# Second attention: one PSUM bank moves from the projections' ring to the ring of the turned probabilities, once the compressed branch's blocks are made

## The chip, the core and the metric

The kernel runs on one core of a Trainium2 chip. The metric is the device time of one execution in microseconds (us), the median of several runs. The core's engines work side by side and meet through semaphores: TensorE (PE in the profile; its weight loads are listed apart as PEld), VectorE (DVE), ScalarE (ACT), GpSimd (POOL) and the DMA queues, most of which SyncE (SP) issues. TensorE writes its results to PSUM, which has eight banks of 128 x 512 float32 here, b0 to b7; VectorE and ScalarE read them from there.

## The reference

Two transformer blocks on 512 tokens of width 1024, in float32. The first has a chunkwise mLSTM and a stick-breaking attention, mixed by gates, then a squared-ReLU MLP. The second is an attention with three branches (16 heads of 64 in 4 key groups); this is the part that the change touches. Cut to what matters:

```
def nsa_mixer(h, w_in, w_out, k_pos, k_w1, k_w2, v_pos, v_w1, v_w2, table):
    q, kv, g, z = split_cols(h @ w_in, [NSA_WIDTH, 6 * NSA_KV_WIDTH, 3 * H, 3 * NSA_WIDTH])
    k_c, v_c, k_s, v_s, k_w, v_w = [a.reshape(B, S, G, dh) for a in jnp.split(kv, 6, axis=-1)]
    gates = jax.nn.sigmoid(g).reshape(B, S, 3, H, 1)
    zs = jax.nn.silu(z).reshape(B, S, 3, H, dh)
    kc = compress_kv(k_c, k_pos, k_w1, k_w2)          # 31 blocks of 32 tokens: silu(flat @ w1) @ w2
    vc = compress_kv(v_c, v_pos, v_w1, v_w2)
    o_cmp, p_cmp = nsa_compressed(q, kc, vc, table)   # softmax over the 31 blocks
    sel = select_blocks(p_cmp, S)                     # the top min(16, 8) of 8 blocks: all
    o_slc = nsa_selected(q, k_s, v_s, sel, table)     # causal softmax with a bias by distance
    o_win = nsa_window(q, k_w, v_w, table)            # the same over a window of 512
    o = jnp.stack([o_cmp, o_slc, o_win], axis=2)
    y = jnp.sum(gates * o * zs, axis=2).reshape(B, S, NSA_WIDTH)
    return y @ w_out
```

The result is normalised, scaled and added to the block's input.

## The kernel before

Every weight product is split for accuracy: weights and activations are each held as a high part (float32r) and a low part, and a product is three matmuls, high by high, high by low and low by high (L332 to L334 and L365 to L367). Weights stream through `Weights._load` (L164): a DMA into `wr`, a cast to `wh` on ScalarE (L171), and the low part `wl` by VectorE or, from load 142 on, by GpSimd (L173).

The kernel runs in stages: the first mixer, the MLP, and `nsa` (L781), the second attention, which starts at about 875 us of the profiled execution. In `nsa` TensorE and GpSimd run in the order in which the program is written (L1392); VectorE, ScalarE and SyncE are put in order by the scheduler.

`nsa` divides the eight PSUM banks among four rings at L788. A ring hands out its banks in turn; a tile in a bank may be written by TensorE only once the last reader of the tile before it in that bank is done.

- `bank`, b0, b1, b7: the projections (`pj`, L792) and, as `mx` (L797), the compressed branch's small products: `cmp_middle`, `cmp_output`, `cmp_scores` (L1039) and `cmp_flip` (L1072).
- `sc`, b2 and b3: the score blocks of the selected and the window branch (L1211).
- `tp`, b4 and b5: the turned probabilities (`Unit.flip`, L1223), the turned gate rows (`gate_flip`, L1128), the gates spread over the rows (`gate_scale`, L1139) and the compressed branch's output (`finish`, L1086).
- `av`, b6: probabilities by values (`Unit.mix`, L1239).

`attention` (L1258) walks through 8 head pairs, 2 branches, 2 heads and 4 query blocks: 128 steps. A step issues two score matmuls (L1213, L1214). VectorE adds the bias and takes the row's minimum (L1216), and ScalarE takes the exponent (L1219). Two steps later TensorE turns the block by 1 to 4 transposes against the identity into a `tp` bank (L1233), ScalarE copies the high part to `ptall` (L1236) and VectorE the low part (L292). When two query blocks are turned, and two steps have passed, `mix` multiplies them by the values (L1249); its result is copied to `t` by ScalarE (L1255) and added up by VectorE (L292).

Between these pieces `Filler` (L187) issues other work on TensorE in portions: the projections that later heads need (`gen_t`, 8 portions of three matmuls, L332 to L334), read after the last portion by ScalarE and VectorE (L991 and L289 for `z`; L874 and L289 for queries; L852 for keys). `early` (L1005) makes the compressed keys and values first; its last lines are

```
                yield from weave(keys(2), {2: middle, 5: lambda: output(1)})
                spread_values(0)
                spread_values(1)
```

after which the compressed branch's blocks are made. `combine(p)` (L1168) then goes through the head pairs: three `z` projections each, and at set portions the compressed branch's scores (`cmp_scores`, half a group at a time), their softmax and `cmp_flip`. `gate_flip`, `gate_scale` and `finish` are jobs that the filler issues as soon as their inputs are ready. After the last head pair the remaining flips, mixes and jobs are issued, and then the output projection (L365 to L367).

Of the kernel before, what the change touches and what calls it, by code (L numbers as in the profile page):

```python
# [8 lines left out]
F32 = mybir.dt.float32  # L9
# [6 lines left out]
T = 512  # L16
# [235 lines left out]
def tile_blocks(ctx, tc, x, xt, wts, prm, cst, table, post_g, w2k, w2v, out):  # L252
# [6 lines left out]
    banks = ctx.enter_context(tc.tile_pool(name="banks", bufs=1, space=PSUM))  # L259

    def ring(*ids):
        turn = [0]

        def take():
            i = ids[turn[0] % len(ids)]
            turn[0] += 1
            return banks.tile([128, T], F32, name=f"b{i}", tag=f"b{i}", bufs=1)
        return take
# [512 lines left out]
    def nsa(x2, ssq2):  # L781
# [3 lines left out]
        kst, qst = {}, {}  # L785
        with ExitStack() as pts:
            pt = pts.enter_context(tc.tile_pool(name="pt", bufs=1))
            bank, sc, tp, av = ring(0, 1, 7), ring(2, 3), ring(4, 5), ring(6)  # L788

            opened, when, used = [0], [0], [0]  # L790

# [2 lines left out]
                when[0] = fill.ticks  # L794
                return bank()

            mx = bank  # L797

            acts = [act_tiles(kt) for kt in range(KT)]

# [64 lines left out]
            def keys(gq):  # L865
                return gen_t(pj, acts, keys_evac(gq))
# [12 lines left out]
            def queries(m):  # L879
                return gen_t(pj, acts, queries_evac(m))  # L880
# [48 lines left out]
            def cmp_hidden(Fs, st):  # L929
                hp = pj()  # L930
                for k4 in range(4):
                    wh, wl = W.next()
                    Fh, Fl = Fs[k4]
                    for jj in range(4):
                        a = wh[:, 256 * jj:256 * jj + 256]
                        b = wl[:, 256 * jj:256 * jj + 256]
                        o = hp[:, 0:256]
                        pe.matmul(o, Fh[:, jj, :], a, start=(k4 == 0 and jj == 0), stop=False)
                        pe.matmul(o, Fh[:, jj, :], b, start=False, stop=False)
                        pe.matmul(o, Fl[:, jj, :], a, start=False, stop=(k4 == 3 and jj == 3))  # L940
                    if k4 < 3:
                        yield 1300.0
                th = pt.tile([128, 256], F32, name="th", tag="z", bufs=ZB)
                s.activation(th, hp[:, 0:256], AF.Tanh, scale=0.5)
                stt(th, th, 1.0, hp[:, 0:256], OP.add, OP.mult)
                st["th"] = th
                yield 1300.0

            def cmp_middle(th):
                pst = mx()  # L950
                for k in range(2):
                    pe.transpose(pst[:, 128 * k:128 * k + 128], th[:, 128 * k:128 * k + 128], ident)
                hT = pt.tile([128, 256], F32, name="hT", tag="z", bufs=ZB)
                ts(hT, pst[:, 0:256], 0.5)
                return hT
# [3 lines left out]
            def cmp_output(i, hT, w2):  # L959
                o = mx()  # L960
                for k in range(2):
                    if i == 0:
                        pe.matmul(o[:, 0:128], w2[:, k, :], hT[:, 128 * k:128 * k + 128],
                                  start=(k == 0), stop=(k == 1))
                    else:
                        pe.matmul(o[:, 0:64], hT[:, 128 * k:128 * k + 128], w2[:, k, :],
                                  start=(k == 0), stop=(k == 1))
                if i == 0:
                    hi_lo(kc[:, :, 0, :], kc[:, :, 1, :], o[:, 0:128].rearrange("p (g c) -> p g c", g=4))
                else:  # L970
                    vc = w2t[:, 1, 0:64]
                    v.tensor_copy(vc, o[:, 0:64])
                    tc.keep_in_program_order(g.memset(vcb, 0.0))
                    pct["v"] = vc

            def spread_values(gq):
                vc = pct["v"]
                for r in range(4):
                    o = vcb[32 * r:32 * r + 32, gq, r // 2, 64 * (r % 2):64 * (r % 2) + 64]
                    (s.copy, v.tensor_copy)[r % 2](o, vc[32 * gq:32 * gq + 32, :])  # L980

            def project(p, br):
                if (p, br) in zt:
                    return
                while live[0] == ZB:
                    yield None
                live[0] += 1
                z = pt.tile([128, T], F32, name="z", tag="z", bufs=ZB)

                def evac(ps):  # L990
                    s.activation(z, ps, AF.Tanh, scale=0.5)  # L991
                    stt(z, z, 1.0, ps, OP.add, OP.mult)
                yield from gen_t(pj, acts, evac)
                zt[p, br] = z
# [4 lines left out]
            def weave(gen, hooks):  # L999
                for k, ns in enumerate(gen):  # L1000
                    yield ns
                    if k in hooks:
                        hooks[k]()

            def early():  # L1005
                st = {}

                def middle():
                    st["hT"] = cmp_middle(st["th"])

                def output(i):
                    cmp_output(i, st["hT"], st[i])
                Fs, st[0] = yield from compress(0)
                yield from both(cmp_hidden(Fs, st), project(0, 0))
                Fs, st[1] = yield from compress(1, ({2: middle}, {2: lambda: output(0)}))
                started[0] = True
                yield from both(cmp_hidden(Fs, st), queries(4))
                yield from weave(keys(2), {2: middle, 5: lambda: output(1)})
                spread_values(0)
                spread_values(1)  # L1020

            def both(a, b):
                for k, ns in enumerate(b):
                    yield ns
                    if k % 2 == 1:
                        try:
                            yield next(a)
                        except StopIteration:
                            pass
                yield from a  # L1030
# [321 lines left out]
            for br in range(2):  # L1352
                values(br)
            load_near(0)
            fill.add(early(), 57200.0)
            attention(fill)
            fill.finish()
# [34 lines left out]
    with tc.manual_schedule(engines={mybir.EngineType.PE, mybir.EngineType.Pool}):  # L1392
        nsa(xb, sums2)
# [55 lines left out]
```

## Time and profile before

| what | value |
|---|---|
| median of 3 runs | 1371.41 us (1369.96 to 1372.78) |
| the profiled execution's own time | 1371.08 us |
| its span in the profile | 1369.4 us |
| PE busy | 1324.5 us (97%) |
| PEld busy | 1091.6 us (80%) |
| DVE, ACT, POOL busy | 720.9, 655.6, 273.8 us |
| chain of waits that ended last | PE 70%, issue 15%, DVE 8%, ACT 4% |

The profile's instruction rows give the start in us from the span's start, the duration, the engine, the line of the program, the operation, out<-in by the program's names, the shapes and how many were merged into the row; in brackets stands the engine's idle time just before, with what ended it. Matmuls are pipelined: the ends of those rows are modelled and lie behind the start of the next one, so a wait of TensorE is read best from start to start. [...]

### The profile page before, as it was taken

The numbers are of one execution on the slowest core, as the hardware profiler recorded it, in microseconds if no ns is written. First come the engines' busy times: TensorE is split into PE (matmuls) and PEld (weight loads), VectorE is DVE, ScalarE is ACT, GpSimd is POOL, SyncE is SP. The second block draws the span as 40 slices with busy tenths as digits, with TensorE's granted clock in tenths as the row PEclk, the third lists the DMA queues.
The fourth block names the chain that finished last, engine by engine and source line by source line (L and its number), as shares of the span: only waits on it lengthen the run. The fifth ranks groups of instructions, "written<-read, shape, count | busy, mean of one in ns | idle before, by whom it ended". The sixth has DMA issues, their size and how long they took to land.

```text
span 1369.4 us, 17872 instructions
## 1 busy us (share of the span) xinstructions
PE 1324.5 (97%) x6670; PEld 1091.6 (80%) x6670; DVE 720.9 (53%) x1354; ACT 655.6 (48%) x1281; POOL 273.8 (20%) x243
## 2 busy tenths in 40 slices
PE   9999999999999999999999999999889999999998
PEld 7977887777786888888888888888767788888776
DVE  4589435656567535342233322544775766665623
ACT  6588624544434316351135512345556566665532
POOL 0023101110101000000000000145536344335342
PEclk9999999999999999999999999999999999999999
DMA  7411231223131424862333224313313112222132
GB/s 236 139 46 48 77 93 51 88 62 93 47 107 47 154 62 133 122 186 92 95 102 96 93 92 125 126 60 124 100 49 113 50 62 65 68 62 62 47 109 77
DMA packets 40694, 125.30 MB, mean 92 GB/s; under 512 B 4528, under 2 KB 9184, under 8 KB 40352
## 3 DMA queue, kind: packets, MB, share of 16 engines
q1 hardware_dynamic: 39696, 119.98, 28.0%
q0 software_dynamic: 912, 4.19, 2.3%
q8 instruction: 52, 0.85, 0.3%
q14 instruction: 34, 0.28, 0.1%
HBM read 115.77 MB, written 8.39 MB: 91 GB/s over the span
## 4 chain that ended last, share of the span: by engine, by line
PE 70%; issue 15%; DVE 8%; ACT 4%; POOL 2%; DMA 1%; POOLq 0%; DVEq 0%; SPq 0%; ACTq 0%
PE b L365 10%; PE b L367 10%; PE b L366 10%; PE b L332 10%; PE b L333 9%; PE b L334 9%; PE b L1249 2%; PE b L1233 2%; PE b L1213 1%; PE b L1214 1%; PE b L828 1%; DVE ptall L292 1%; ACT P L1219 1%; DVE b L1216 1%; POOL ssr L292 1%
## 5 line engine op out<-in xcount | busy, mean ns | idle before, releaser
L171 ACT CAST wh<-wr 128x1024 fp32r<-128x1024 f32 (+3 forms) x204 | 207.7, 1019 | 404.6 <-PE b L367 225.1
L332 PE MATMUL b<-ah,wh 128*128 128x512 f32 x808 | 332.1, 411 | 2.6 <-ACT w2t L852 2.2
L173 DVE TENSOR_TENSOR wl<-wr,wh 128x1024 fp32r<-128x1024 f32 (+2 forms) x142 | 169.4, 1194 | 297.1 <-ACT wh L171 296.6
L334 PE MATMUL b<-ah,wl 128*128 128x512 f32 x808 | 317.4, 393 | 0.0
L333 PE MATMUL b<-al,wh 128*128 128x512 f32 x808 | 317.2, 393 | 0.0
L173 POOL TENSOR_TENSOR wl<-wr,wh 128x1024 fp32r<-128x1024 f32 (+1 forms) x62 | 141.6, 2289 | 190.3 <-ACT wh L171 166.3
L334 PEld LDWEIGHTS b<-ah,wl 128*128 128x128 f32 x808 | 152.3, 189 | 32.6
L332 PEld LDWEIGHTS b<-ah,wh 128*128 128x128 f32 x808 | 152.8, 189 | 30.3 <-ACT w2t L852 2.5
L333 PEld LDWEIGHTS b<-al,wh 128*128 128x128 f32 x808 | 153.0, 189 | 25.5 <-issue 1.9
L365 PE MATMUL b<-wh,ah 128*128 128x512 f32 (+3 forms) x352 | 126.1, 360 | 1.9 <-ACT wh L171 1.9
L366 PE MATMUL b<-wl,ah 128*128 128x512 f32 (+3 forms) x352 | 125.8, 357 | 0.0
L367 PE MATMUL b<-wh,al 128*128 128x512 f32 (+3 forms) x352 | 125.8, 357 | 0.0
L1219 ACT ACTIVATE P<-b,nm 128x128 f32<-128x128 f32 (+3 forms) x128 | 67.6, 528 | 77.8 <-DVE nm L1216 73.7
L367 PE MATMUL b<-wh,hl 128*128 128x512 f32 x256 | 101.2, 396 | 0.0
L366 PE MATMUL b<-wl,hh 128*128 128x512 f32 x256 | 101.2, 395 | 0.0
L365 PE MATMUL b<-wh,hh 128*128 128x512 f32 x256 | 101.2, 395 | 0.0
L292 DVE TENSOR_TENSOR ptall<-b,ptall 128x128 fp32r<-128x128 f32 (+3 forms) x128 | 62.4, 489 | 65.1 <-ACT ptall L1236 64.3
L1216 DVE CUSTOM_DVE_ANT_0 b<-b,bt 128x128 f32<-128x128 f32 (+3 forms) x128 | 63.2, 495 | 28.0 <-PE b L1214 27.7
L365 PEld LDWEIGHTS b<-wh,ah 128*128 128x128 f32 x352 | 66.6, 190 | 9.8 <-ACT wh L171 2.1
L367 PEld LDWEIGHTS b<-wh,al 128*128 128x128 f32 x352 | 66.7, 189 | 8.5 <-DVE al L289 0.3
L366 PEld LDWEIGHTS b<-wl,ah 128*128 128x128 f32 x352 | 66.8, 190 | 8.2
L292 POOL TENSOR_TENSOR rsr<-rsm,mhalf 128x2 f32<-128x2 f32 (+1 forms) x3 | 2.4, 806 | 336.4 <-DVE rsm L286 336.4
(301 smaller groups left out, 2153.6 us busy)
## 6 DMA issues: line engine op xcount, KB each, us to landing
wr<-in_wts_dram SPq DMA_DIRECT2D x188, 512.0 KB, 3.6
bt_d<-tr POOLq DMA_DIRECT2D x4, 768.0 KB, 21.6
wr<-in_wts_dram SPq DMA_DIRECT2D x8, 280.0 KB, 2.6
xk<-in_xt_dram SPq DMA_DIRECT2D x8, 256.0 KB, 3.9
xn<-in_x_dram SPq DMA_DIRECT2D x4, 512.0 KB, 4.7
xbig<-in_x_dram SPq DMA_DIRECT2D x1, 2048.0 KB, 9.8
x_d<-xbig SPq DMA_DIRECT2D x8, 256.0 KB, 2.8
bt<-bt_d SPq DMA_DIRECT2D x8, 256.0 KB, 3.2
```

Of the source, the lines that this page charges most:

```text
L171: nc.scalar.copy(hi, raw)
L173: eng.tensor_tensor(lo, raw, hi.bitcast(F32), OP.subtract)
L292: (eng or v).tensor_tensor(out_, a, b, op)
L332: pe.matmul(o, a, ah, start=(kt == 0), stop=False)
L333: pe.matmul(o, a, al, start=False, stop=False)
L334: pe.matmul(o, b, ah, start=False, stop=(kt == KT - 1))
L365: pe.matmul(o, ah[:, tsl], a, start=(kk == 0 and k == 0), stop=False)
L366: pe.matmul(o, ah[:, tsl], b, start=False, stop=False)
L367: W.last = pe.matmul(o, al[:, tsl], a, start=False, stop=end)
L1216: v.tensor_tensor_reduce(S[:, 0:n], S[:, 0:n], self.bt[:, h % 2, 512 - n:512], 1.0, -NEG, OP.add, OP.min, nm)
L1219: latest[0] = s.activation(P[:, 0:n], S[:, 0:n], AF.Exp, bias=nm, scale=-1.0, accum_out=self.dn[:, tb, br, h % 2:h % 2 + 1])
L1233: pe.transpose(pst[:, 128 * sb:128 * sb + 128], P[:, 128 * sb:128 * sb + 128], ident)
```

## The change

```
-            bank, sc, tp, av = ring(0, 1, 7), ring(2, 3), ring(4, 5), ring(6)
+            sc, av = ring(2, 3), ring(6)
+            ids = {"bank": [0, 1, 7], "tp": [4, 5]}
+            given = {"bank": -1, "tp": -1}
+
+            def from_ring(name):
+                i = given[name] = (given[name] + 1) % len(ids[name])
+                return banks.tile([128, T], F32, name=f"b{ids[name][i]}", tag=f"b{ids[name][i]}", bufs=1)
+
+            def bank():
+                return from_ring("bank")
+
+            def tp():
+                return from_ring("tp")
+
+            def regroup():
+                last = ids["bank"][given["bank"]]
+                ids["bank"] = [0, 1]
+                given["bank"] = last if last < 2 else 0
+                ids["tp"] = [4, 5, 7]
...
-            mx = bank
+            def mx():
+                return bank() if len(ids["bank"]) == 3 else tp()
...
                 yield from weave(keys(2), {2: middle, 5: lambda: output(1)})
                 spread_values(0)
                 spread_values(1)
+                regroup()
```

Until `regroup` runs, at the end of `early`, the rings are as before. From then on the projections have two banks, b0 and b1; the `tp` ring has three, b4, b5 and b7, and also takes the compressed branch's scores and turned blocks (`cmp_scores`, `cmp_flip`). The number of instructions and, on TensorE, GpSimd and SyncE, their order are unchanged. On ScalarE and on VectorE one instruction moves ahead of a neighbour, at one place some ten us after `early`: the copy of a turned block (L1236) ahead of an exponent (L1219), and that block's low part (L292) between the two adds of a compressed score. Everything else is the bank that a tile lies in.

TensorE's order at the end of `early` before: the last portion of the keys of group 2 (tile 8641 in b0), a turned block, then the next projection, tile 8746; the digit behind b is the bank, the number behind it the tile.

```order
L334 MATMUL b0_8641<-ah7_6869,wl_8473 128x512
L1233 MATMUL b5_8726<-ident_65,P_8620 128x128 x2
L332 MATMUL b0_8746<-ah0_6855,wh_8533 128x512
L333 MATMUL b0_8746<-al0_6856,wh_8533 128x512
L334 MATMUL b0_8746<-ah0_6855,wl_8534 128x512
```

The same place with the change (line numbers from the rings on are 18 to 20 higher):

```order
L334 MATMUL b0_8641<-ah7_6869,wl_8473 128x512
L1253 MATMUL b5_8726<-ident_65,P_8620 128x128 x2
L332 MATMUL b1_8746<-ah0_6855,wh_8533 128x512
L333 MATMUL b1_8746<-al0_6856,wh_8533 128x512
L334 MATMUL b1_8746<-ah0_6855,wl_8534 128x512
```

Before, tile 8746 takes the bank of the keys that were finished just ahead of it; now it takes b1, whose last tile was the compressed values' turned hidden layer.

TensorE before at the first two `finish` products (L1088, of head pairs 0 and 1), with one portion of a projection and one turned block between them:

```order
L1088 MATMUL b5_9109<-pct_9093,vcb_6871 128x512
L332 MATMUL b7_9077<-ah3_6861,wh_8742 128x512
L333 MATMUL b7_9077<-al3_6862,wh_8742 128x512
L334 MATMUL b7_9077<-ah3_6861,wl_8743 128x512
L1233 MATMUL b4_9116<-ident_65,P_9013 128x128 x2
L1088 MATMUL b5_9121<-pct_9093,vcb_6871 128x512
```

and with the change:

```order
L1108 MATMUL b4_9109<-pct_9093,vcb_6871 128x512
L332 MATMUL b0_9077<-ah3_6861,wh_8742 128x512
L333 MATMUL b0_9077<-al3_6862,wh_8742 128x512
L334 MATMUL b0_9077<-ah3_6861,wl_8743 128x512
L1253 MATMUL b5_9116<-ident_65,P_9013 128x128 x2
L1108 MATMUL b7_9121<-pct_9093,vcb_6871 128x512
```

Before, the second product reuses b5 after one other `tp` tile; now two other `tp` tiles lie between two uses of a bank.

TensorE before at the attention's end: the last two turned blocks, the turned gate rows of head pair 7 (L1131), the first half of the last mix, the first spread gate (L1141), the mix's second half:

```order
L1233 MATMUL b5_11471<-ident_65,P_11406 128x128 x3
L1233 MATMUL b4_11477<-ident_65,P_11431 128x128 x4
L1131 MATMUL b5_11484<-ident_65,gz_6877 128x128 x4
L1249 MATMUL b6_11491<-ptall_6876,vst_6874 128x256
L1249 MATMUL b6_11491<-ptall_6876,vst_6874 128x128
L1249 MATMUL b6_11491<-ptall_6876,vst_6874 128x256
L1249 MATMUL b6_11491<-ptall_6876,vst_6874 128x128
L1141 MATMUL b4_11496<-gT_11489,gsel_6879 128x512
L1249 MATMUL b6_11491<-ptall_6876,vst_6874 128x256 x3
```

and with the change:

```order
L1253 MATMUL b7_11471<-ident_65,P_11406 128x128 x3
L1253 MATMUL b4_11477<-ident_65,P_11431 128x128 x4
L1151 MATMUL b5_11484<-ident_65,gz_6877 128x128 x4
L1269 MATMUL b6_11491<-ptall_6876,vst_6874 128x256
L1269 MATMUL b6_11491<-ptall_6876,vst_6874 128x128
L1269 MATMUL b6_11491<-ptall_6876,vst_6874 128x256
L1269 MATMUL b6_11491<-ptall_6876,vst_6874 128x128
L1161 MATMUL b7_11496<-gT_11489,gsel_6879 128x512
L1269 MATMUL b6_11491<-ptall_6876,vst_6874 128x256 x3
```

The gate rows' tile 11484 follows tile 11471 in b5 before; now b5 last held an earlier turned block, and 11471 lies in b7.

## Rows read from the trace of the kernel before

**Rows 1.** Waits of TensorE, 1054 to 1318 us: line, releaser, total us, times, longest.
```profile
PE b L332 <- ACT w2t L852: 2.2, 1, 2.2
PE b L1233 <- DVE ptall L292: 1.9, 5, 0.7
PE b L1131 <- DVE ptall L292: 1.8, 1, 1.8
PE b L1088 <- DVE z L292: 0.9, 1, 0.9
PE b L1141 <- DVE ptall L292: 0.8, 1, 0.8
PE b L1141 <- DVE z L292: 0.4, 1, 0.4
```
**Rows 2.** Windows: length, busy of PE, PEld, DVE, ACT, POOL, PEclk, DMA share, GB/s.
```profile
1054.00:1318.00 264.00, 255.44 (x1453) 214.11 (x1452) 170.29 (x428) 159.23 (x394) 102.29 (x59) 0.99 0.20 58
1056.90:1062.30 5.40, 5.40 (x35) 4.77 (x35) 5.22 (x8) 4.70 (x11) 1.69 (x1) 1.00 0.36 102
1316.00:1320.00 4.00, 4.00 (x17) 3.50 (x17) 1.86 (x3) 0.58 (x1) 3.15 (x3) 0.71 0.43 98
```
**Rows 3.** Timeline of TensorE around the wait at 1102 us.
```profile
1101.12 0.39 PE L333 MATMUL b<-al,wh 128*128 128x512 f32 x1
1101.35 0.40 PE L334 MATMUL b<-ah,wl 128*128 128x512 f32 x1
1102.42 0.33 PE L1233 MATMUL b<-ident,P 128*128 128x128 f32 x1 [0.67 <-DVE ptall L292]
1102.51 0.48 PE L1141 MATMUL b<-gT,gsel 128*128 128x512 f32 x1
```
**Rows 4.** Timeline of TensorE at the end of `early` and seven us later.
```profile
1054.05 0.38 PE L1233 MATMUL b<-ident,P 128*128 128x128 f32 x2
1056.66 0.50 PE L332 MATMUL b<-ah,wh 128*128 128x512 f32 x1 [2.24 <-ACT w2t L852]
...
1063.44 0.57 PE L1249 MATMUL b<-ptall,vst 128*128 128x256 f32 x4
```
**Rows 5.** Timeline of ScalarE at the same place.
```profile
1055.08 1.04 ACT L171 CAST wh<-wr 128x1024 fp32r<-128x1024 f32 x1
1056.03 0.58 ACT L852 COPY w2t<-b 128x512 f32<-128x512 f32 x1
```
**Rows 6.** Timeline of VectorE: the add that empties b6.
```profile
1061.62 0.68 DVE L292 TENSOR_TENSOR t<-t,b 64x512 f32<-64x512 f32 x1
```
**Rows 7.** Timeline of TensorE at the attention's end.
```profile
1310.86 0.94 PE L1233 MATMUL b<-ident,P 128*128 128x128 f32 x7
1313.64 0.66 PE L1131 MATMUL b<-ident,gz 128*128 128x128 f32 x4 [1.84 <-DVE ptall L292]
1314.05 0.65 PE L1249 MATMUL b<-ptall,vst 128*128 128x256 f32 x4
1314.97 0.79 PE L1141 MATMUL b<-gT,gsel 128*128 128x512 f32 x1 [0.27 <-ACT gT L1133]
...
1318.66 0.40 PE L365 MATMUL b<-wh,yh 128*128 128x512 f32 x1
```
**Rows 8.** Timelines of VectorE and ScalarE at the attention's end.
```profile
1312.31 0.69 DVE L292 TENSOR_TENSOR t<-t,b 64x512 f32<-64x512 f32 x1
1313.03 1.16 DVE L292 TENSOR_TENSOR ptall<-b,ptall 128x384 fp32r<-128x384 f32 x2
...
1311.85 0.95 ACT L1236 CAST ptall<-b 128x384 fp32r<-128x384 f32 x2
...
1314.33 0.59 ACT L1133 CAST gT<-b 128x512 fp32r<-128x512 f32 x1 [1.53 <-PE b L1131]
```
**Rows 9.** Timelines of VectorE and TensorE: a projection's last read, that bank's next opening.
```profile
1133.53 0.69 DVE L289 SCALAR_TENSOR_TENSOR q<-b,q 64x512 fp32r<-64x512 f32 x1
...
1139.31 0.48 PE L332 MATMUL b<-ah,wh 128*128 128x512 f32 x1
```

## The prediction

> **What bounds the kernel now.** I read the windows first, then TensorE's waits, then the timeline around each wait. In the stretch that the change can touch, from the end of `early` to the output projection, TensorE is busy in 255.4 of 264 us, VectorE in 170 and ScalarE in 159 [rows 2]. So TensorE's own order sets the pace, and only what makes it wait can be won. Its waits are few [rows 1]: ten in six groups, 8.0 us of idle time together, all of them for ScalarE or VectorE to finish with a tile. The reader is to see that each first line named is one that opens a PSUM bank: the first portion of a projection (L332), a turned block (L1233), turned gate rows (L1131), a `finish` product (L1088) or a spread gate (L1141). The score blocks (L1213) and the mixes (L1249) are not in the list. Nine of the ten stand in the `tp` ring of two banks, and the tenth in the projections' ring.
>
> The idle time of a row is smaller than what the wait costs. A matmul of 512 columns lasts 0.39 us in the rows, but the next starts 0.23 us after it [rows 3]; seven transposes take 0.94 us, so 0.11 us from one to the next with a last one of 0.27 [rows 7]. In both cases 0.16 us of the earlier row overlaps what would have followed. A wait therefore costs its idle time and 0.16 us. The check is the wait at 1102.42: 1.07 us after the start before it instead of 0.23, which is 0.84, against 0.67 + 0.16.
>
> **The change part by part.** No instruction is added or taken away and TensorE's order stands, so the sum is made of waits that go, shrink or appear.
>
> 1. The projection after `early`. It waits 2.24 us because the ring's turn gives it the bank of the keys just finished, whose copy (L852) stands behind a weight cast on ScalarE and ends at 1056.61 [rows 4, 5]. Cost 2.40 us. With b1, long read, it can follow the transposes. What is late next is the mix at 1063.44: it opens b6, which VectorE frees at 1062.30 [rows 4, 6]. VectorE is busy 5.22 of the 5.40 us ahead of that [rows 2], with the keys' low parts, which wait for the same copy as before, so it won't be earlier. The mix can start 0.05 us later, at 1062.35, and the gain is 1.1 us. Bounds: 1.1, if VectorE keeps its queue, and 2.4, if it makes room; I take 1.1, since the row shows no room.
>
> 2. Five turned blocks, 1.9 us idle, 1.9 + 5 x 0.16 = 2.7 us. With three banks each has a tile's time more. One of the five is not won: the block at 1102.42 gets b4, and the spread gate 0.09 us behind it gets b5 and so the same low part to wait for [rows 3]. Of that wait's 0.83 us only 0.09 remains. Sum 2.7 - 0.83 + 0.09 = 1.96.
>
> 3. One `finish` product, 0.9 + 0.16 = 1.06 us [rows 1]: it waited for VectorE to multiply the `finish` product before it, in the same bank; now it takes b7.
>
> 4. Two spread gates, 0.8 + 0.4 + 2 x 0.16 = 1.52 us [rows 1], won in the same way.
>
> 5. The end. The turned gate rows wait for the low part of a block that shares their bank, 1.84 us [rows 7]. With the change they follow the seven transposes: start 1310.86 + 7 x 0.11 = 1311.63, end of the four at about 1312.3. What is late next is the first half of the mix, since VectorE frees b6 at 1312.31 + 0.69 = 1313.00 [rows 8]: start 1313.05 instead of 1314.05. ScalarE is free at 1312.80 and copies the gate rows in 0.59, until 1313.39 [rows 8]; the spread gate follows at 1313.5, the second half of the mix needs the last low part, ready at 1313.03 + 1.16 = 1314.19, for its last four matmuls, and ends with the second spread gate at about 1314.7. The fourth matmul of the output projection, at 1318.66 before [rows 7], comes at 1314.95 + 0.70 = 1315.65: 3.0 us won. [...] With the change 0.75 us of waiting is left there, as much as in waits of rows 1 after which the clock did not fall: over the whole stretch its mean is 0.99, and the hundredth, 2.6 us of the 264, is about the end's own. Bounds: 1.3 if the clock falls all the same, 3.0 if not; I take 3.0.
>
> Nothing is costed for the rest, with these covers. A projection's evacuation has 5.1 us to spare with two banks at the tightest of 25 openings: the queries read last at 1134.22 are followed in b1 by the opening at 1139.31 [rows 9]. The cost if that cover is gone is rival C. The compressed scores and turned blocks now pass through `tp`; each holds a bank for a few us more, beside a third bank, and behind them in TensorE's queue stand portions and scores for which ScalarE waits: rival B. The instruction that moves on ScalarE and VectorE issues nothing and goes past one neighbour.
>
> [...]
>
> Sum: 1.1 + 1.96 + 1.06 + 1.52 + 3.0 = 8.6 us. The profiled execution took 1371.08 us (span 1369.4 and 1.7 around it), 0.3 under the median, so I take the sum off the median: 1371.4 - 8.6 = **1362.8 us**. Gains add up because VectorE and ScalarE, busy less than two thirds of the stretch, are mostly started by TensorE and move forward with it.
>
> **The rivals.**
>
> A. The waits are passed on. As at 1102 us, the next instruction may need what the same queue on VectorE delivers late, and a third bank would only move the wait. For it: the row itself, and that VectorE is full for whole stretches like 1056.9 to 1062.3 [rows 2]. Against it: after the other waits the next bank needed is one read earlier. Then the eight waits of steps 2 to 4 bring 0.09 us each, 0.7, with 1.1 for the first and 1.3 at the end: 3.1 us, 1368.3 us.
>
> B. Slower through the compressed branch: its eight scores and four turned blocks wait in `tp` behind low parts that VectorE delivers late, where in the old ring they found banks read long before. If each waits as the block at 1102 us did, 12 x 0.84 = 10 us, and a few flips wait behind them for another 2: 1371.4 - 8.6 + 12 = 1375 us. It decides once VectorE is later than two turned blocks, about 4 us, at such a place. Against it: the `tp` waits of now are at most 0.87 us with two banks.
>
> C. Slower through the projections: 25 openings that wait as the `finish` product did, 1.03 us each, 26 us: 1371.4 - 8.6 + 26 = 1389 us. It decides when an evacuation lasts 5 us longer than in rows 9. [...] The trace shows the clock to stay at 0.99 through the waits of now [rows 2].
>
> That the change does not do what it says I leave out: the banks in TensorE's order are as the ring says.
>
> **How the numbers follow.** Forecast 0.76, A 0.16, B 0.05, C 0.03. The forecast's own range comes from its bounds: step 1 may bring 1.3 more, the end 1.7 less, and some waits of steps 2 to 4 (4.5 us) may be passed on: 1361 to 1366. To hold 8 in 10 the range reaches toward A and leaves half of it, B and C outside: 1360.5 to 1367.5. A measurement of this kernel can tell 0.2%, 2.7 us, from no change. The forecast lies beyond that, A (3.1 us) on its edge: 0.08 of it faster, 0.08 the same. Of B 0.03 is slower, 0.02 the same, C is slower. Faster 0.84, same 0.10, slower 0.06.
>
> **What would show it.** In the changed profile the waits of L332, L1088 and L1131 (by their old numbers) are gone from TensorE's list between `early` and the output projection, and what is left there is under 3 us; the mix seven us after `early` is late for b6, and a spread gate waits where the block at 1102 us did; the clock stays at 1.00 around the attention's end. Wrong would be: new waits at compressed scores (B) or at first portions of projections (C), or a list with as much idle time under other lines (A).

## The result, and the profile after

| | before | changed |
|---|---|---|
| median | 1372.01 us (1369.96 to 1372.78, 4 runs) | 1362.43 us (1362.11 to 1363.05, 4 runs) |
| ratio | | 0.9931, 95% interval 0.9919 to 0.9944 |
| span of the profiled execution | 1369.4 us | 1360.4 us |
| mean granted clock | 0.993 | 0.995 |

The changed kernel is 9.6 us faster; the forecast was 8.6 less than 1371.4, 1362.8 us. The two profiled executions differ by 9.0 us (1371.08 and 1362.11), which is what the starts below add up to; the medians differ by more, with four runs of the kernel before spread over 2.8 us. Lines 788 and later have moved: L1233 (turned block) is now L1253, L1213 (score) L1233, L1249 (mix) L1269, L1131 (gate rows) L1151, L1141 (spread gate) L1161, L1088 (product of `finish`) L1108, and the compressed scores and turned blocks are L1066 and L1096.

TensorE's list of waits from `early` to the output projection, in the columns of [rows 1], has two lines left, 2.7 us:

```profile
PE b L1269 <- DVE t L292: 2.1, 2, 1.3
PE b L1161 <- DVE ptall L292: 0.6, 1, 0.6
```

The list of the kernel before has seven lines, with eleven waits and 8.3 us. [rows 1] shows six of them; the seventh is the first spread gate at the end, which waits for its own input ([rows 7] has it at 1314.97):

```profile
PE b L1141 <- ACT gT L1133: 0.3, 1, 0.3
```

The windows of that stretch and of the attention's end, against [rows 2]: nine microseconds less for the same matmuls (1453 and 1454 records), and the clock at the end (PEclk, the share of TensorE's full speed that was granted) is 1.00 instead of 0.71.

```profile
1054.00:1309.00 255.00, 252.25 (x1454) 213.11 (x1453) 169.41 (x427) 158.76 (x394) 101.30 (x58) 1.00 0.20 60
...
1307.00:1311.00 4.00, 3.99 (x23) 3.43 (x24) 3.01 (x5) 0.63 (x2) 2.15 (x2) 1.00 0.31 82
```

At the end of `early` [rows 4] the projection follows the transposes, and the mix seven microseconds later waits. Below it is the add on VectorE that empties its bank [rows 6]: it ends at 1062.39, and the mix starts at 1062.44, as worked out (1062.35).

```profile
1054.10 0.38 PE L1253 MATMUL b<-ident,P 128*128 128x128 f32 x2
1054.24 0.48 PE L332 MATMUL b<-ah,wh 128*128 128x512 f32 x1
...
1062.44 0.67 PE L1269 MATMUL b<-ptall,vst 128*128 128x256 f32 x4 [1.28 <-DVE t L292]
```

```profile
1061.71 0.68 DVE L292 TENSOR_TENSOR t<-t,b 64x512 f32<-64x512 f32 x1
```

Where the block of 1102.42 waited [rows 3], the block no longer waits, and the spread gate behind it does. Nothing is won (0.83 us at the block, 0.84 lost again at the gate); the prediction, which worked out that this wait is passed on, left 0.09:

```profile
1098.95 0.27 PE L1253 MATMUL b<-ident,P 128*128 128x128 f32 x1
1099.87 0.47 PE L1161 MATMUL b<-gT,gsel 128*128 128x512 f32 x1 [0.65 <-DVE ptall L292]
```

The attention's end, against [rows 7]: the gate rows start 0.78 us after the seven transposes do, where 2.78 us passed before, and the mix is the one that waits.

```profile
1304.63 0.95 PE L1253 MATMUL b<-ident,P 128*128 128x128 f32 x7
1305.41 0.60 PE L1151 MATMUL b<-ident,gz 128*128 128x128 f32 x4
1306.82 0.67 PE L1269 MATMUL b<-ptall,vst 128*128 128x256 f32 x4 [0.81 <-DVE t L292]
1307.50 0.47 PE L1161 MATMUL b<-gT,gsel 128*128 128x512 f32 x1
1307.81 1.04 PE L1269 MATMUL b<-ptall,vst 128*128 128x256 f32 x8
1308.68 0.44 PE L1161 MATMUL b<-gT,gsel 128*128 128x512 f32 x1
...
1309.67 0.39 PE L365 MATMUL b<-wh,yh 128*128 128x512 f32 x1
```

TensorE runs the same matmuls in the same order in both kernels, so each start can be set against its own start before. In the stretch the difference grows from nothing (-0.05 us at 1054) to 9.01 us, in some fifteen steps:

| step of the prediction | forecast, us | measured, us, from starts in the two profiles |
|---|---|---|
| 1 projection after `early` | 1.1 | 2.48 won, 1.55 given back at the mix: 0.93 |
| 2 five turned blocks | 1.96 | 0.59 + 0.83 - 0.84 + 0.53 + 0.35 + 0.43 = 1.89 |
| 3 product of `finish` | 1.06 | 1.13 |
| 4 two spread gates | 1.52 | 1.01 + 0.63, less 0.18 at a compressed score 3 us behind the first: 1.46 |
| not counted: 1184.84 and 1225.72 | 0 | 0.25 + 0.37 = 0.62 |
| 5 the end | 3.0 | 2.80 |
| sum | 8.6 | 8.83; the rest up to 9.06 is steps under 0.06 |

### The profile page after: what moved, and what is told of

The parts are those of the page before. It is cut to its first block, busy times and chain, and to the rows that moved or that the text cites. A ratio compares the mean times of both kernels' runs of the same rounds, so it can differ in the third digit from the quotient of the medians.

```text
span 1360.4 us, 17887 instructions
## 1 busy us (share of the span) xinstructions
PE 1321.1 (97%) x6670; PEld 1090.4 (80%) x6670; DVE 719.8 (53%) x1354; ACT 655.8 (48%) x1281; POOL 273.9 (20%) x243
## 4 chain that ended last, share of the span: by engine, by line
PE 72%; issue 15%; DVE 7%; ACT 3%; POOL 2%; DMA 1%; POOLq 0%; DVEq 0%; SPq 0%; ACTq 0%
PE b L332 10%; PE b L333 10%; PE b L334 10%; PE b L367 9%; PE b L365 9%; PE b L366 9%; PE b L1269 3%; PE b L1253 2%; PE b L1233 1%; PE b L1234 1%; PE b L847 1%; DMA xk<-in_xt_dram 1%; POOL ssr L292 1%; POOL ke L630 1%; DVE kl L292 1%
## 5 line engine op out<-in xcount | busy, mean ns | idle before, releaser
L332 PE MATMUL b<-ah,wh 128*128 128x512 f32 x808 | 332.0, 411 | 0.4 <-DVE q L289 0.3
L332 PEld LDWEIGHTS b<-ah,wh 128*128 128x128 f32 x808 | 152.6, 189 | 28.0 <-issue 1.9
L292 DVE TENSOR_TENSOR ptall<-b,ptall 128x128 fp32r<-128x128 f32 (+3 forms) x128 | 62.4, 489 | 63.7 <-ACT ptall L1256 63.0
L1236 DVE CUSTOM_DVE_ANT_0 b<-b,bt 128x128 f32<-128x128 f32 (+3 forms) x128 | 63.2, 494 | 27.2 <-PE b L1234 26.3
L292 POOL TENSOR_TENSOR rsr<-rsm,mhalf 128x2 f32<-128x2 f32 (+1 forms) x3 | 2.4, 806 | 334.8 <-DVE rsm L286 334.8
```

The lines of the kernel that those rows point to most:

```text
L292: (eng or v).tensor_tensor(out_, a, b, op)
L332: pe.matmul(o, a, ah, start=(kt == 0), stop=False)
L1236: v.tensor_tensor_reduce(S[:, 0:n], S[:, 0:n], self.bt[:, h % 2, 512 - n:512], 1.0, -NEG, OP.add, OP.min, nm)
```

## The experiments

Theory: the gain is the third bank's, because a turned block's bank is emptied by ScalarE and then by VectorE, the queue that is late (it ends nine of the ten waits of [rows 1]); the move of the compressed blocks is what makes it affordable for the projections. Rivals: the move alone does it; the projections pay; the gain would come wherever the bank goes. (The score blocks' ring was not tried: its blocks wait for nothing in this stretch.) "Before" is timed beside each run. Each run's kernel has its own line numbers, at most three off those of the changed kernel: L1063 in e3, for one, is the compressed scores and L1093 their turned blocks.

**e1: the projections' turn alone.** The rings of before; the only change is one turn at the end of `early`.

```diff
 def regroup():
-    last = ids["bank"][given["bank"]]
-    ids["bank"] = [0, 1]
-    given["bank"] = last if last < 2 else 0
-    ids["tp"] = [4, 5, 7]
+    given["bank"] += 1
 def mx():
-    return bank() if len(ids["bank"]) == 3 else tp()
+    return bank()
```

> The kernel before (three banks for the projections, two for turned blocks, the compressed branch's blocks still in the projections' ring), with one thing changed: the projections' ring is advanced by one turn at the end of `early`, so that the next projection does not open the bank of the keys just finished. Theory (step 1 of the prediction): that wait of 2.24 us goes, and the mix seven us later then waits about 1.3 us for b6, so the net gain on the kernel before is 1.0 us (the changed kernel showed a shift of 0.95 there), some 1371.0 us; all the waits of the turned blocks, the product of `finish`, the spread gates and the end stay, 8.1 us by the changed kernel's total. Rival: VectorE's queue makes room and the whole 2.4 us is won, 1369.6. Rival: the wait is only moved to another opening, gain under 0.3.

Measured: 1369.45 us against 1371.17, ratio 0.9988 (0.9980 to 0.9996), 0.5 to 2.7 us faster. From start to start the projection wins 2.48 and the mix gives back 1.56: 0.92, the theory's term. All the other waits of [rows 1] are there, with their sizes. So this tenth of the gain needs no third bank. The median's difference is 1.7 us, and the rest of it goes with the clock: in the profiled execution it stays at 1.00 behind the wait at the end, where it is 0.50 before (last section), and 6 of the 12 runs have a mean clock of 0.995, none of the 17 runs of before beside them. Whether the turn brings that about is not shown.

**e2: third bank, compressed blocks stay with the projections.**

```diff
 def mx():
-    return bank() if len(ids["bank"]) == 3 else tp()
+    return bank()
```

> The changed kernel, but the compressed branch's scores and turned blocks stay in the projections' ring, which now has two banks. Theory: two banks are enough for the projections only while nothing else opens a bank between them. With each compressed tile in between, the next projection opens the bank that the projection just before it has filled. By the times of the changed kernel's profile, at 14 openings in this order the bank's last reading would end 0.2 to 3.2 us late, 31.6 us in all. If each delay is paid in full the time is 1362.4 + 31.6 = 1394 us; if the readings move forward a little where several fall close together, 1385 to 1394. Rival: the readings have room to come earlier, and it stays under 1367 as the changed kernel. Waits should be named at L332 for VectorE's z.

Measured: 1403.04 us, ratio 1.0234 (1.0217 to 1.0250). The place and the mechanism are the theory's, the price was too low. The waits of the stretch:

```profile
PE b L332 <- DVE z L289: 25.6, 12, 2.8
PE b L1096 <- issue: 3.1, 1, 3.1
PE b L1269 <- DVE t L292: 2.2, 2, 1.3
```

"Issue" means that the profile names no releaser; the block of that line starts 0.11 us after VectorE's last read of the queries, so it too seems to wait for a bank of the projections. The first two lines are 28.7 us of idle, with 13 x 0.16 some 30.8, close to the 31.6 of lateness. But against the changed kernel the same stretch lost 42.9 us. The other 12 go with a mean clock of 0.95 from 1054 to 1352 us, where the changed kernel has 1.00. Behind the first wait of this kind, 2.56 us, the window says 0.50:

```profile
1066.00:1068.40 2.40, 0.00 (x0) 0.00 (x0) 1.25 (x4) 1.99 (x6) 1.13 (x1) 0.94 0.00 0
1068.40:1071.50 3.10, 3.09 (x8) 2.47 (x9) 0.42 (x1) 0.37 (x1) 1.23 (x1) 0.50 0.30 46
```

So the move of the compressed blocks, which by itself wins nothing (e3), is the condition for all the rest.

**e3: compressed blocks moved, no third bank.**

```diff
 def regroup():
-    ids["bank"] = [0, 1] ...
-    ids["tp"] = [4, 5, 7]
+    ids["mx"] = []
 def mx():
-    return bank() if len(ids["bank"]) == 3 else tp()
+    return tp() if "mx" in ids else bank()
```

> Only the compressed branch's blocks move to the turned blocks' ring, which keeps its two banks, and the projections keep three. Theory: the price that the third bank has to cover. By the times of the changed kernel's profile the openings in this order find their bank read late by 21.9 us in all (the first projection 2.4, a turned block at 1059.9 us 3.1, the compressed scores and turned blocks 6.5 together, the end 2.4), so 1362.4 + 21.9 = 1384 us, about 12 us over the kernel before; new waits stand at the compressed scores and turned blocks and at the block behind the first of them. Rival, as rival B priced it: 12 waits of 0.84 us, 1372 + 10 = 1382, with no wait over 1 us among them. Rival: the blocks find banks read in time, 1372.

Measured: 1377.23 us, ratio 1.0043 (1.0031 to 1.0055), 6 us slower than before where 10 to 12 were expected. Three of twelve compressed blocks wait:

```profile
PE b L1063 <- ACT gT L1150: 2.8, 1, 2.8
PE b L332 <- ACT w2t L868: 2.3, 1, 2.3
PE b L1093 <- issue: 2.1, 1, 2.1
...
PE b L1093 <- DVE z L292: 0.4, 1, 0.4
...
```

The expectation added up late readings as if each were paid. A wait of 2.8 us makes the next openings late too, and their banks are then read in time: the block at 1059.9, 3.1 us late on paper, found its bank free, since TensorE had just waited 2.3 us and went on at a mean clock of 0.68 (1055.76 to 1061.16, last section). The release named in the first line is the copy of the gate rows, two tiles ahead in the same ring. Beside the changed kernel the third bank is thus worth about 15 us once the compressed blocks are there. Of that, 2.5 us stand between the end of `early` and the mix behind it, from the first projection's wait and the clock of 0.68 after it; e1 takes that wait away without a third bank.

**e4: two banks again for the drain at the attention's end.**

```diff
+last = ids["tp"][given["tp"]]
+ids["tp"] = [4, 5]
+given["tp"] = 1 if last == 5 else 0
 while pend_flip or pend_mix:
     tick[0] += 1
```

> The changed kernel, with the turned blocks' ring put back to its two old banks for the drain at the attention's end alone (the last eight turned blocks, gate rows and spread gates). Theory (step 5): the gate rows wait about 1.9 us again for the low part of the block that shares their bank, and the granted clock falls in the microseconds behind it, so 2.8 us come back: 1362.4 + 2.8 = 1365.2 us, and the mean clock from 1308 to 1312 us is near 0.7. Rival: the clock does not depend on this wait, 1.0 us of late start and no more, at most 1.3: 1363.4 to 1363.7, clock 1.00.

Measured: 1365.71 us, ratio 0.9957 (0.9945 to 0.9969) against 0.9931 for the changed kernel. Up to the end the starts are those of the changed kernel; then the wait of 1.84 us is back, and the clock falls behind it, from 1.00 (1306 to 1309.5 us) to 0.50 (1310.5 to 1312.5 us):

```profile
1308.38 0.66 PE L1151 MATMUL b<-ident,gz 128*128 128x128 f32 x4 [1.84 <-DVE ptall L292]
1308.80 0.66 PE L1269 MATMUL b<-ptall,vst 128*128 128x256 f32 x4
1309.72 0.66 PE L1161 MATMUL b<-gT,gsel 128*128 128x512 f32 x1 [0.27 <-ACT gT L1153]
1310.17 1.80 PE L1269 MATMUL b<-ptall,vst 128*128 128x256 f32 x8
```

Against before nothing is won there any more (5.22 us ahead of it, 5.19 behind), where the changed kernel won 2.80. The window from 1308 to 1312 us has a mean clock of 0.74, as expected. So the wait of step 5 is the two banks', and in this profile the clock falls behind it; in e1's profile it does not fall behind the same wait (last section).

**a1: the changed kernel again, beside e5, e8 and e9.**

> The changed kernel itself, once more on the chip of the three runs beside it, so that they can be compared with it directly. Theory: 0.9931 of the kernel before, as it was measured first (0.9919 to 0.9944), and the spread of its runs is smaller than that of the kernel before, since the wait at the attention's end, after which the clock fell in some executions and not in others, is gone: clock 0.995 or 0.996 in all of them. Rival: the clock varies as much as before, 0.993 to 0.995.

Measured: 1362.46 us, ratio 0.9933 (0.9919 to 0.9946). The spread did not shrink: 1360.27 to 1363.08 against 1370.19 to 1372.64, with clocks of 0.994 and 0.995. That part of the theory is refuted: ahead of 1054 us, where nothing was changed, TensorE's starts in the two profiles of the changed kernel already differ by 0.9 us.

**e5: the bank passes at the start of `early`.**

```diff
 def early():
+    regroup()
     st = {}
 ...
     spread_values(1)
-    regroup()
```

> The changed kernel, but the bank passes at the start of `early` instead of its end, where the turned blocks, the gate rows and their part of TensorE wait 6.3 us for a bank with two banks. Theory: it is slower. In `early` the compressed branch's hidden product holds one of the projections' banks for several portions, so with two banks its opening and the next projection wait for the evacuation of the bank just filled. By the times of the changed kernel's profile four openings find their bank read late by 16.9 us (6.8, 2.6, 6.3, 1.2), the waits that the third bank takes away there give back at most 6.3, and each is followed by another tile that needs the same queue: 1362.4 + 10 to 17 = 1372 to 1379 us. Rival: the hidden product's openings have room behind them, and the third bank wins the 6.3 us and the half-clock stretch behind the wait of 4.0 us: 1354 us.

Measured: 1376.66 us, ratio 1.0041 (1.0028 to 1.0054), within the theory's range. The waits from 950 to 1062 us:

```profile
PE b L957 <- DVE z L289: 11.7, 2, 6.6
PE b L332 <- DVE q L289: 3.4, 1, 3.4
PE b L1233 <- ACT P L1239: 3.1, 2, 2.7
PE b L332 <- DVE z L289: 2.3, 1, 2.3
PE b L1151 <- DVE gz L292: 1.9, 1, 1.9
...
```

L957 is the first matmul of the hidden product. It opens while the other bank is in use and the one it gets is not yet read. So it matters, too, when the bank passes: here it could go once the long accumulation was closed.

**e8: the bank goes to the mixes.**

```diff
-sc, av = ring(2, 3), ring(6)
+sc = ring(2, 3)          # av() takes its bank from ids["av"], [6] at first
 def regroup():
-    ids["tp"] = [4, 5, 7]
+    ids["av"] = [6, 7]
```

> The changed kernel, but the bank goes to the mixes (two banks, 6 and 7), and the turned blocks keep two; the compressed branch's blocks are in the turned blocks' ring as in the changed kernel. Theory: a third bank is worth most where a bank's tile is read last by the queue that is latest, and that is the turned blocks' ring; the mixes waited once in 264 us. It wins the waits of the first projection and of the mix behind it, 1.4 us more than the changed kernel there, and leaves all waits of the turned blocks. From the run with the compressed blocks in the two-bank ring (5.9 us over the kernel before, of which 2.3 + 0.16 are the first projection's wait): 1371.2 + 5.9 - 2.5 - 1 = 1372 to 1376 us, waits at L1066, L1096 and L1151. Rival: the mixes' bank is what holds the flow back, and it is as fast as the changed kernel, under 1365.

Measured: 1380.14 us, ratio 1.0069 (1.0057 to 1.0082): slower than before, and by more than expected. The mix no longer waits at the end of `early`; the block ahead of it does, for 3.05 us, since VectorE is just as late for its bank, and from 1062 to 1066 us the clock is 0.50:

```profile
1062.27 1.11 PE L1256 MATMUL b<-ident,P 128*128 128x128 f32 x4 [3.05 <-DVE ptall L292]
1063.03 0.78 PE L332 MATMUL b<-ah,wh 128*128 128x512 f32 x1
...
1066.17 0.63 PE L332 MATMUL b<-ah,wh 128*128 128x512 f32 x1
```

No first portion of a projection (L332) is in its list of waits: with the compressed blocks out of their ring, two banks are enough for the projections. The compressed blocks lie in a ring of two banks here as in e3 and wait as there (2.8, 2.1 and 0.5 us), so most of the loss against before is e3's; from 1054 us to the output projection this profile loses 3.1 us more than e3's, with the bank given away. A second bank for the mixes without the move was not run.

**e6: one bank for the projections, four for the turned blocks.**

```diff
 def regroup():
-    ids["bank"] = [0, 1] ...
-    ids["tp"] = [4, 5, 7]
+    ids["bank"], given["bank"] = [0], 0
+    ids["tp"] = [4, 5, 7, 1]
```

> The changed kernel with one more bank taken from the projections: they have a single bank from the end of `early` on, and the turned blocks four. It prices rival C, where the projections wait at each of 25 openings. Theory: each opening then waits for the reading of the portion that has just ended, by the times of the changed kernel's profile 1.2 to 5.8 us late, 62.8 us in all at 25 openings, 2.5 us each and not the 1.03 us of rival C; where idle times are that long the granted clock falls in some of them, as it did in the run with the compressed blocks in the projections' ring (1.0 us at half clock behind a wait of 2.6 us, 33.6 us lost for 31.6 of lateness): 1362.4 + 63 to 75 = 1425 to 1437 us, waits at L332 for VectorE's z and q. The turned blocks' waits should be no fewer than with three banks (2.7 us left then, of which the spread gate's 0.65 may go). Rival: the portions are so spread between other work that one bank costs 1.03 us per opening, 26 us: 1388 us.

(The 33.6 us named there is e2's loss against before; against the changed kernel it is 42.9.) Measured: 1440.53 us, ratio 1.0509 (1.0491 to 1.0526), 3.5 us above the theory's range. All 25 openings wait:

```profile
PE b L332 <- DVE z L289: 39.7, 20, 2.8
PE b L332 <- DVE q L289: 12.7, 3, 5.7
PE b L332 <- ACT w2t L869: 3.1, 2, 2.3
PE b L1267 <- DVE t L292: 0.8, 1, 0.8
```

They are 55.5 us of idle, 2.2 each. The spans differ by 75.4 us; 55.5 + 25 x 0.16 is 59.5, and the other 16 go with a mean clock of 0.94 in the stretch (1054 to 1385 us). The spread gate's wait of 0.65 is gone.

**e9: two of the three remaining waits.**

```diff
-self.o = av()
+self.o = sc() if (self.h, self.br) == (15, 1) else av()
 ...
-tt(kl[...], src, kh[same, :].bitcast(F32), OP.subtract)
+tt(kl[...], src, kh[same, :].bitcast(F32), OP.subtract, eng=g if gq == 2 else v)
```

> The changed kernel with two of its three remaining waits taken away. The last mix opens a score bank, which nothing needs any more, instead of b6 (0.81 us of idle at the end); and the low parts of the keys made at the end of `early` are computed on GpSimd, which is idle there for 8.7 us, instead of VectorE, so that VectorE frees b6 earlier for the mix at 1062.44 (1.28 us of idle). Theory: 1.28 + 0.16 us at the mix and 0.3 to 0.5 at the end, where the spread gate then waits for the gate rows' copy and the second half of the mix for the last low part: 1.8 us less than the changed kernel beside it, 1360.6 us. Rival: GpSimd's subtractions and VectorE slow each other, or the next weights' low parts come late, and it is no faster or slower. Rival: the mix then waits for the copy on ScalarE, gain under 0.6.

Measured: 1361.69 us beside 1362.46, ratios to before 0.9928 (0.9916 to 0.9941) and 0.9933 (0.9919 to 0.9946): the lowest median, but not told apart from the changed kernel. In the profiles the mix at the end of `early` waits no more, 1.55 us, but three later instructions give half of that back: a product of `finish` at 1088.2 starts 0.28 late, a spread gate at 1099.9 0.19, and a turned block at 1182.2 0.29; up to the output projection 0.8 is left. At the end nothing is won: the mix starts without waiting and the spread gate behind it waits 1.09 us instead.

```profile
1305.72 0.60 PE L1152 MATMUL b<-ident,gz 128*128 128x128 f32 x4
1306.08 0.65 PE L1270 MATMUL b<-ptall,vst 128*128 128x256 f32 x4
1307.82 0.47 PE L1162 MATMUL b<-gT,gsel 128*128 128x512 f32 x1 [1.09 <-DVE ptall L292]
```

## Why the prediction was right

It named the waits that go, sized each by start to start (idle and 0.16 us), and asked at each what is late next. Its count of ten waits and 8.0 us leaves out the eleventh, 0.3 us, but no term rests on the count: that wait lies inside step 5, which works from starts.

- Step 1 stood on VectorE being full ahead of the mix. The mix started 0.09 us from where it was put, and e1 shows the term by itself.
- Steps 2 to 4 came within 0.1 us each. The block at 1102 us was rightly left out; it is the only one of the eight waits of these steps that was passed on, so rival A, all of them passed on, falls.
- Two delays that the prediction did not have brought 0.62, at a turned block and at a product of `finish`. By the rows before, their matmuls start 0.12 and 0.10 us behind the modelled end of the one ahead, and the list of waits leaves out times as short as these; only starts show them. The other terms together came 0.4 short; that the sum came closer than its parts is luck.
- Step 5 came 0.2 short. The mix came 2.19 us behind the start of the transposes, as worked out. The spread gate was put 2.64 behind and came 2.87 behind: the prediction let it wait for the copy of the gate rows, and it waits for its own bank, b7, which VectorE's low part frees. e9, where nothing else is ahead of it, shows that wait openly. The clock's part came: from the first spread gate to the fourth matmul of the output projection, 3.69 us before and 2.17 with the change (1307.50 to 1309.67), at a mean clock of 0.71 (1316 to 1320 us) and of 1.00 (1307 to 1311 us). The prediction's two bounds for the end, 1.3 and 3.0, leave 1.7 us to the clock; that was the author's estimate, no run shows it, and what the profiles show is 1.5 us, between the kernel before and e1 (last section). The prediction took it that the clock falls because of this wait. In e4's profile it falls behind it (0.53), in e1's it stays at 1.00 behind the same wait, so this part, 1.5 of the forecast's 8.6 us, came in part by luck. The prediction's check on it, that the hundredth missing from the mean clock of 0.99 is the end's own, rests on a rounded figure and shows nothing.
- Rival B was right in kind: with two banks the compressed blocks do wait (e3). It priced twelve waits of 0.84; there were three, 5.3 us together. With the third bank one of the twelve is 0.18 late.
- Rival C was wrong for this change, and its price was too low: 2.2 us of idle per opening (e6), not 1.03, and a mean clock of 0.94 on top. The slack of 5.1 us [rows 9] held: no first portion of a projection waits in the changed kernel. In e2, e5 and e6 an opening waits for the evacuation of a tile before it in its bank (25.6 us at L332, 11.7 at L957, 55.5 in all); in the changed kernel two banks are enough for the projections.

The parts are far from additive: the third bank without the move costs 32 us (e2), the move without the third bank 6 (e3), both together win 9.6.

## What to carry to other kernels

Here the spare bank paid in the ring whose tiles are read last by the latest queue (9.6 us). Give it there only after asking how many other tiles open banks in the ring that lends it, and which accumulation holds one for long. Cost a wait by starts, not by idle time, and follow each one to the next instruction that needs the same queue: one in eight was only passed on here, but at the attention's end every wait that was taken away uncovered the next (1.84 us at the gate rows, then 0.81 at the mix, then 1.09 at the spread gate). Late readings worked out on a profile may not be added up where they stand close together (e3); the first one that is paid covers the next.

## What the runs showed of the hardware

The same wait need not cost the same clock. In three profiles the end has the same idle times, 1.84 us ahead of the gate rows and 0.27 ahead of the spread gate, and TensorE was at full clock and busy ahead of them: 1.00, and 11.00 of the 11 us from 1300 to 1311, in the kernel before and in e1; in e4 its rows follow each other without idle time from 1303.81 to the seven transposes at 1305.60, and the clock from 1306 to 1308.5 us is 1.00. These are three microseconds behind, in the kernel before, in e4 and in e1, each cut to the same place in the work:

```profile
1315.00:1318.00 3.00, 3.00 (x11) 2.81 (x12) 0.75 (x2) 0.58 (x1) 1.35 (x2) 0.50 0.00 0
```

```profile
1309.70:1312.70 3.00, 2.98 (x11) 2.73 (x12) 0.85 (x2) 0.58 (x1) 1.44 (x2) 0.53 0.00 0
```

```profile
1315.30:1318.30 3.00, 3.00 (x17) 2.66 (x18) 2.00 (x3) 0.58 (x1) 1.66 (x2) 1.00 0.38 76
```

Two are at 0.50 and 0.53 of full speed and do 11 matmuls, the third stays at 1.00 and does 17. From the first spread gate to the fourth matmul of the output projection it is 3.69 us before [rows 7] and 2.19 in e1 (1315.26 to 1317.45), 1.5 us less. The end of `early` shows the same the other way round: behind the first projection's wait of 2.24 us the clock before stays at 1.00 [rows 2], and behind the same wait of 2.26 us, over the same length, it is 0.68 in e3:

```profile
1055.76:1061.16 5.40, 5.40 (x26) 4.70 (x25) 5.22 (x8) 4.69 (x11) 1.70 (x1) 0.68 0.36 102
```

So by these profiles 1.5 of the 2.80 us won at the end is won only in an execution whose clock would have fallen there. How many of the runs that is, is not known: e1's twelve go from 1366.88 us to 1371.90, those with a mean clock of 0.995 took at most 1369.7 and those with 0.993 at least 1370.6, but a run's mean clock does not tell where it fell (from 2 to 100 us, where nothing was changed, it is 0.98 in the profile of the kernel before and 1.00 in the changed kernel's). What decides it in one of them is left open; no run varied it alone.
